# Hybrid decoder layer: product order in seven-product pairs, a smaller set of them, the store of h, and the spread of h's transposes

## The chip, the cores and the metric

The kernel runs on one core of a Trainium2 chip. The metric is the device time of one execution in microseconds (us), the median of several runs. Lower is better.

## The reference

The layer takes x of 256 rows by 2048 channels in float32 and computes

- `merged = sigmoid(g_A) * Up_A(FoX(xn)) + sigmoid(g_B) * Up_B(NSA(xn))`, with `xn = RMSNorm(x)` and two attention mixers FoX and NSA, all projected from xn by one matrix;
- `h = x + merged @ w_out` (w_out is 2048 x 2048);
- `y = h + (silu(hn @ w_gate) * (hn @ w_up)) @ w_down`, with `hn = RMSNorm(h)` and a hidden width of 5632.

The change lies in the second and third line. The first, which takes the first 640 us, it doesn't touch.

## The kernel before

**Precision.** Every matmul operand is split into hi (float32r, written by ScalarE with a copy) and lo (the remainder, written by VectorE with a subtraction). One product of a 128-wide block is then three matmuls of 128x512: hi by hi, hi by lo, lo by hi (lines 1066 to 1068, in `mac`).

**Pairs and units.** From the output projection on, the work is a list of units. A unit gives 256 rows by 1024 columns of output; it runs over `Pair`s, each with two 128-row blocks of the weight and the matching two blocks of the activation. That is a 2x2 by 2x2 block product. A plain pair (`mm_plain`) does it with eight block products into four sums (m2, m3, m4, c), so 24 matmuls; `mid` is called between its halves. A seven-product pair (`mm_seven`) uses the Winograd form: seven block products m1 to m7, so 21 matmuls, of which m1, m2 and m3 take plain blocks of the weight (part 0 of the split) and m5, m7, m6 and m4 take sums of blocks (part 1). The order of the seven is written out by hand: m1, m5, m7, m6, m2, m4, m3. m1, m5, m6 and m7 have four PSUM banks ("acc"), the others four more ("tp", printed as m in the profile). Transposes use acc banks too, when they are free.

**What the other engines do for a pair.** `Pair.load` issues two DMAs of 512 KB on SyncE's queue. `Pair.split` makes the parts: for a seven-product pair part 0 is three additions on VectorE (the sums, lines 1035 to 1038), then hi (line 1043, ScalarE) and lo (line 1044, VectorE) of three blocks; part 1 is hi and lo of the four sums. A plain pair has one part, hi and lo of four blocks. There are four part buffers, so the split of a part waits until TensorE has used the part four before it.

**After the last seven-product pair of a unit** `combine` reads m1 on ScalarE (line 1099) and m6, m7, m5 on VectorE (lines 1100 to 1103; m6 first) and so frees those banks. In the output units and the last down units `add_rows` then starts four DMAs on GpSimd's queue that add x (or h) to the four tiles in place (line 1135). After the unit's last pair `last` adds m2, m4, m3 and c to the tiles on VectorE (line 1112), and calls `done`.

**The two output units** (i = 0 and 1, 1024 columns of h each). Unit 0 takes the pairs in the order 1, 3, 0, 2, 5, 4, 6, 7, unit 1 from 0 to 7; pairs 0, 2 and 4 (`SW`) are seven-product ones. `done` is `h_evac`: the sum of squares of each tile, the store of h to `hacc` in DRAM (line 1162, on SyncE), and after unit 1 the second norm's scale `rh`, whose power runs on GpSimd (line 291).

**Transposes of h.** The gate/up units need h transposed, in eight pairs `hT[kp]`, made by `put_h`: four transposes of 128x128 on TensorE (line 996), then `put_seven` for kp 0, 2, 4 (lines 975 to 988) or `put_plain` for the others (hi on line 967, lo on line 968). Hooks say when: `(j, 0)` is before pair j of a unit and before the splits that are issued there, `(j, 1)` is between the halves of pair j. In unit 1 `(5, 0)` made kp 0 and 1 and `(5, 1)` kp 2 and 3; in the first gate/up unit `(3, 0)` made 4 and 5 and `(3, 1)` made 6 and 7. That first gate/up unit has pairs 0 and 2 as seven-product ones (`SH[:2]`), and pair 4 plain, on operands laid out for seven.

**The rest.** Eleven gate/up units in three groups (`GROUPS`), each group with two down units; down units of the first two groups accumulate into `hacc` by GpSimd's DMAs. The last group's first down unit takes its pairs in the order 0, 1, 2, 4, 3, 5, 6, 7, of which 0, 2 and 4 are seven-product ones.

**Order.** Nothing reorders the instructions: each engine runs its own in the order of the program. Before each pair the main loop calls the hook `pre`, then `run_ffn`, which issues loads and splits as far as buffers allow (three raw buffers, and parts of this and the next pairs up to `PARTS = 4`), then the products, then `combine` or `last`:

```python
if i >= ffn and ch.pre: ch.pre()
...
run_ffn(i)
...
ch.mm(ch)
...
if ch.done: ch.done()
```

Of the kernel before, what the change touches and what calls it, by code (L numbers as in the profile page):

```python
# [8 lines left out]
F32 = mybir.dt.float32  # L9
F32R = mybir.dt.float32r  # L10
AF = mybir.ActivationFunctionType
ALU = mybir.AluOpType
AX = mybir.AxisListType

P = 128
D = 2048
KB = D // P
T = 256
# [35 lines left out]
def hybrid_block(ctx: ExitStack, tc: tile.TileContext, x, norm_attn, w_in, fox_f_bias,  # L54
# [3 lines left out]
    nc = tc.nc  # L58
# [33 lines left out]
    def wk(shape, tag, bufs, dt=F32):  # L92
        pool = keep if tag in ("qs", "sm") else work
        return pool.tile(shape, dt, tag=tag, name=nm(tag), bufs=bufs)

    def bank(tag):
        tag = "acc" if tag == "acc" else "m"
        return psum.tile([P, 512], F32, tag=tag, name=nm(tag), bufs=4)
# [187 lines left out]
    def rstd_from(dst, ssq, n):  # L286

        w = ssq.shape[-1]
        v = wk([P, 16], "sm", 11)
        nc.vector.tensor_scalar(v[:, :w], ssq, 1.0 / n, EPS, op0=ALU.mult, op1=ALU.add)  # L290
        nc.gpsimd.tensor_tensor(dst, v[:, :w], nhalf[:, :w], op=ALU.pow)

    def row_ssq(dst, src):
        junk = wk([P, 512], "qs", 4)
        nc.scalar.activation(junk[:, :src.shape[-1]], src, AF.Square, accum_out=dst)
# [586 lines left out]
    mT = [None] * 8  # L882
    mtask, msrc = {}, {}
    SW = (0, 2, 4)
# [49 lines left out]
    def p3(shape, tag, bufs, dt=F32):  # L934
        return pools[3].tile(shape, dt, tag=tag, name=nm(tag), bufs=bufs)

    hacc = dram.tile([T, D], F32, name="hacc")
# [21 lines left out]
    def put_plain(dst, b, gains):  # L959
        if gains is None:  # L960
            d0, d1 = (dst[:, o].rearrange("p k t -> p (k t)") for o in range(2))
            nc.scalar.activation(d0, b, AF.Copy)
            nc.vector.tensor_tensor(d1, b, d0.bitcast(F32), op=ALU.subtract)
            return
        for k in range(2):
            hi, lo, src = dst[:, 0, k], dst[:, 1, k], b[:, k * T:(k + 1) * T]
            nc.scalar.activation(hi, src, AF.Copy, scale=gains[k])
            nc.vector.scalar_tensor_tensor(lo, src, gains[k], hi.bitcast(F32), op0=ALU.mult, op1=ALU.subtract)

    def put_seven(dst, b, gains):  # L970

# [79 lines left out]
    def unit(order, sevens, srcs, act, done, need, hooks=None, add=None):  # L1051


        hooks = hooks or {}
        plain = {(0, 0): "m2", (0, 1): "m3", (1, 0): "m4", (1, 1): "c"}
        total, seen, bk = {}, {}, {}
        for kp in order:
            for k in [f"m{j}" for j in range(1, 8)] if kp in sevens else list(plain.values()) * 2:
                total[k] = total.get(k, 0) + 1

        def mac(key, h, l, hi, lo):
            if key not in bk:
                bk[key] = bank("acc" if key in ("m1", "m5", "m6", "m7") else "tp")
            o, n = bk[key], seen.get(key, 0)
            seen[key] = n + 1
            nc.tensor.matmul(o, h, hi, start=n == 0, stop=False)  # L1066
            nc.tensor.matmul(o, h, lo, start=False, stop=False)  # L1067
            nc.tensor.matmul(o, l, hi, start=False, stop=n + 1 == total[key])  # L1068

        def mm_seven(ch):  # L1070
            a = act(ch.kp)
            o0 = a.shape[2] - 7
            for key, o, part, slot_ in (("m1", 0, 0, 0), ("m5", 3, 1, 0), ("m7", 4, 1, 1), ("m6", 5, 1, 2),
                                        ("m2", 1, 0, 1), ("m4", 2, 1, 3), ("m3", 6, 0, 2)):
                hi, lo = ch.op[part]
                mac(key, a[:, 0, o0 + o], a[:, 1, o0 + o], hi[:, slot_], lo[:, slot_])

        def mm_plain(ch):
            a = act(ch.kp)
            hi, lo = ch.op[0]  # L1080
            for c in range(2):
                if c and ch.mid:
                    ch.mid()
                for t in range(NT):
                    for k in range(2):
                        sl = ((1, 2), (0, 3))[c][k]
                        if a.shape[2] == 8:
                            ah, al = (a[:, o, ((1, 2), (0, 3))[t][k]] for o in range(2))
                        else:
                            ah, al = (a[:, o, k, t * P:(t + 1) * P] for o in range(2))  # L1090
                        mac(plain[t, c], ah, al, hi[:, sl], lo[:, sl])

        sb = {}

        def combine():

            (t1, t3), (u, w) = ([wk([P, 512], "qs", 4) for _ in range(2)], [p3([P, 512], "q2", 5) for _ in range(2)])
            tt, stt = nc.vector.tensor_tensor, nc.vector.scalar_tensor_tensor
            nc.scalar.activation(t1, bk["m1"], AF.Copy)
            tt(u, bk["m6"], t1, op=ALU.add)  # L1100
            tt(t3, bk["m7"], u, op=ALU.add)
            stt(w, bk["m5"], -1.0, t3, op0=ALU.mult, op1=ALU.subtract)
            stt(u, bk["m5"], -1.0, u, op0=ALU.mult, op1=ALU.subtract)
            for k in ("m1", "m5", "m6", "m7"):
                del bk[k]
            sb.update({(0, 0): t1, (0, 1): u, (1, 0): t3, (1, 1): w})
            if add:
                add(sb)

        def last():  # L1110
            for k in ((0, 0), (1, 0), (0, 1), (1, 1)):
                nc.vector.tensor_tensor(sb[k], bk[plain[k]], sb[k], op=ALU.add)
            done(sb)
            bk.clear()

        last7 = max(j for j, kp in enumerate(order) if kp in sevens)
        for j, kp in enumerate(order):
            def fin(j=j):
                if j == last7:
                    combine()  # L1120
                if j == len(order) - 1:
                    last()
            sv = kp in sevens
            pre, mid = hooks.get((j, 0)), hooks.get((j, 1))
            stream.append(Pair(unit, kp, sv, srcs(kp), mm_seven if sv else mm_plain, pre, mid, fin,
                               (lambda kp=kp: need(kp)) if need else None))

    def two(w, r0, c0):
        return lambda kp: [w[r0 + kp * 2 * P:r0 + (kp + 1) * 2 * P, c:c + 512] for c in (c0, c0 + 512)]
# [17 lines left out]
    def put_h(kp):  # L1147
        c = hs[kp // 4]
        k = kp // 2 % 2
        make = lambda kp: p3([P, 2, 8, P], "h7", len(SH), F32R) if kp in SH else p3([P, 2, 2, T], "hp", 8 - len(SH), F32R)  # L1150
        gains = [vecT[:, VF + 2 * kp + o:VF + 2 * kp + o + 1] for o in range(2)]
        hT[kp] = transpose_pair(make, [c[t, k] for t in range(NT)], kp % 2 * 256, kp, SH, gains, "acc")

    def put_hs(*kps):
        return lambda: [put_h(kp) for kp in kps]

    def h_evac(i):
        def done(c):
            hs[i] = dict(c)
            for t, h in ((0, 0), (1, 0), (0, 1), (1, 1)):  # L1160
                row_ssq(hss[:, t, 2 * i + h:2 * i + h + 1], c[t, h])
                nc.sync.dma_start(hacc[t * P:(t + 1) * P, (2 * i + h) * 512:(2 * i + h + 1) * 512], c[t, h])
            if i:
                s2 = wk([P, 16], "sm", 11)
                nc.vector.tensor_reduce(s2[:, :NT], hss, axis=AX.X, op=ALU.add)
                rstd_from(rh, s2[:, :NT], D)
        return done

    for i in range(2):
        unit((1, 3, 0, 2, 5, 4, 6, 7) if i == 0 else range(8), SW, two(w_out, 0, i * 1024), lambda kp: mT[kp], h_evac(i),  # L1170
             None if i else lambda kp: [mtask[j] for j in range(3)],
             {(5, 0): put_hs(0, 1), (5, 1): put_hs(2, 3)} if i else
             {(0, 1): put_m(5), (1, 0): put_m(6), (1, 1): put_m(7)}, add_rows(x, i * 1024))


# [49 lines left out]
    for g, (f0, f1) in enumerate(GROUPS):  # L1225
        n = 2 * (f1 - f0)
        order = list(range(n))
        more = g + 1 < len(GROUPS)

        for f in range(f0 + (1 if g else 0), f1 + (1 if more else 0)):  # L1230
            gate_up(f, transposes(f - 1, 5) if f > f0 + (1 if g else 0) else
                    {(3, 0): put_hs(4, 5), (3, 1): put_hs(6, 7)} if f == 0 else {})
        if more:
            down_unit(g, 0, order, {})
            down_unit(g, 1, order, transposes(f1, at[n]))
        else:
            down_unit(g, 0, [0, 1, 2, 4, 3, 5, 6, 7], transposes(f1 - 1, 4))
            down_unit(g, 1, order, {})
# [118 lines left out]
```

## Time and profile before

| | |
|---|---|
| runs, us | 1444.2, 1441.73, 1445.09 (median 1444.2) |
| profiled execution | 1444.2 us, span 1442.5 us, granted TensorE clock 0.997 |
| instructions | 18073, of them 6748 matmuls |
| moved by DMA | 287.06 MB, 199 GB/s in the mean |
| chain that ended last | TensorE 89%, VectorE 5%, ScalarE 2%, issue 2%, DMA 1% |

The span is from the first instruction to the last. The chain is followed back from the end: at each step to what released the waiting engine. In a row of a timeline the first number is the start in us from the span's start, the second the duration; where the engine stood idle before the instruction for longer, the idle time and what ended it stand in brackets at the end. Matmuls are pipelined, so the next starts before the row of the last ends. PE is TensorE, PEld its weight load, DVE VectorE, ACT ScalarE, POOL GpSimd, SP SyncE.

### The profile page before, as it was taken

The page shows a single profiled execution, that of the slowest core. Times are in us where ns is not written, and L with a number is a line of the kernel's source. Part 1 is how long each engine was busy: PE and PEld are TensorE (multiplying, and loading weights), DVE is VectorE, ACT ScalarE, POOL GpSimd, SP SyncE. Part 2 cuts the span into 40 slices and gives each one's busy share as a digit, 9 for nine tenths or more (in the row PEclk, how much of TensorE's full clock was granted, in tenths as well). Part 3 has the DMA queues.
Part 4 walks back from the last instruction along what each step waited for, and adds up shares of the span by engine and source line. Part 5 has one row for each costly group of instructions (what it writes and reads, how often), then busy time and mean ns, then how long its engine had stood idle before and what let it go on. Part 6 is the DMA issues. An engine that isn't in the chain of part 4 may idle for free.

```text
span 1442.5 us, 18073 instructions
## 1 busy us (share of the span) xinstructions
PE 1428.7 (99%) x6748; PEld 1199.5 (83%) x6748; DVE 1137.3 (79%) x1458; ACT 762.2 (53%) x949; POOL 62.4 (4%) x75
## 2 busy tenths in 40 slices
PE   9999999999999999999999999999999999999998
PEld 7888888999888888888778888888888888888787
DVE  7766766776776646669888999888899988889975
ACT  6466554455667444454655555455555555555542
POOL 2001010000000000000000000010000000000000
PEclk9999999999999999999999999999999999999999
DMA  7576876456443666566865666679565577856585
GB/s 279 175 233 198 268 237 184 129 173 208 148 125 117 195 198 187 180 210 194 257 214 175 205 204 207 201 210 257 175 205 187 197 218 216 257 179 199 179 245 136
DMA packets 156419, 287.06 MB, mean 199 GB/s; under 512 B 9598, under 2 KB 32220, under 8 KB 156204
## 3 DMA queue, kind: packets, MB, share of 16 engines
q1 hardware_dynamic: 151260, 275.87, 60.1%
q0 software_dynamic: 4896, 9.78, 4.0%
q8 instruction: 53, 0.87, 0.2%
q10 hardware_dynamic: 176, 0.27, 0.1%
q14 instruction: 34, 0.28, 0.1%
HBM read 277.48 MB, written 8.40 MB: 198 GB/s over the span
## 4 chain that ended last, share of the span: by engine, by line
PE 89%; DVE 5%; ACT 2%; issue 2%; DMA 1%; POOL 0%; SPq 0%; ACTq 0%; DVEq 0%; POOLq 0%
PE acc L193 12%; PE acc L194 12%; PE acc L195 12%; PE m L1068 12%; PE m L1067 12%; PE m L1066 12%; PE acc L1067 3%; PE acc L1068 3%; PE acc L1066 3%; DVE lo L1044 2%; ACT hi L1043 2%; DMA q<-in_x_dram 1%; DVE sums L1035 1%; PE acc L996 1%; PE m L536 1%
## 5 line engine op out<-in xcount | busy, mean ns | idle before, releaser
L171 DVE TENSOR_TENSOR lo<-raw,hi 128x1024 fp32r<-128x1024 f32 (+5 forms) x229 | 267.5, 1172 | 138.7 <-ACT hi L170 138.5
L1044 DVE TENSOR_TENSOR lo<-raw,hi 128x2048 fp32r<-128x2048 f32 (+1 forms) x148 | 309.1, 2092 | 42.9 <-ACT hi L1043 42.7
L193 PE MATMUL acc<-hi,u 128*128 128x512 f32 (+4 forms) x832 | 322.7, 388 | 0.0
L194 PE MATMUL acc<-lo,u 128*128 128x512 f32 (+4 forms) x832 | 316.9, 381 | 0.4 <-DVE lo L171 0.4
L195 PE MATMUL acc<-hi,u 128*128 128x512 f32 (+4 forms) x832 | 317.0, 381 | 0.0
L170 ACT ACTIVATE hi<-raw 128x1024 fp32r<-128x1024 f32 (+5 forms) x229 | 229.3, 1018 | 151.5 <-PE acc L195 138.9
L1043 ACT ACTIVATE hi<-raw 128x2048 fp32r<-128x2048 f32 (+1 forms) x148 | 257.1, 1752 | 93.0 <-PE m L1068 68.0
L1043 ACT ACTIVATE hi<-sums 128x2048 fp32r<-128x2048 f32 x54 | 103.7, 1920 | 170.1 <-DVE sums L1038 134.2
L195 PEld LDWEIGHTS acc<-hi,u 128*128 128x128 f32 x832 | 156.4, 188 | 27.2
L194 PEld LDWEIGHTS acc<-lo,u 128*128 128x128 f32 x832 | 156.7, 188 | 25.3 <-DVE lo L171 0.9
L193 PEld LDWEIGHTS acc<-hi,u 128*128 128x128 f32 x832 | 156.6, 188 | 24.6 <-ACT hi L170 0.2
L1066 PE MATMUL m<-hi,hp 128*128 128x512 f32 x440 | 172.9, 393 | 0.0
L1068 PE MATMUL m<-hi,hp 128*128 128x512 f32 x440 | 171.5, 390 | 0.0
L1067 PE MATMUL m<-lo,hp 128*128 128x512 f32 x440 | 171.3, 389 | 0.0
L1044 DVE TENSOR_TENSOR lo<-sums,hi 128x2048 fp32r<-128x2048 f32 x54 | 123.7, 2291 | 25.7 <-ACT hi L1043 25.7
L1068 PEld LDWEIGHTS m<-hi,hp 128*128 128x128 f32 x440 | 82.6, 188 | 17.3
L1067 PEld LDWEIGHTS m<-lo,hp 128*128 128x128 f32 x440 | 82.7, 188 | 16.8
L1066 PEld LDWEIGHTS m<-hi,hp 128*128 128x128 f32 x440 | 82.6, 188 | 16.6
L1066 PE MATMUL m<-hi,u 128*128 128x512 f32 x210 | 82.8, 394 | 0.0
L1068 PE MATMUL m<-hi,u 128*128 128x512 f32 x210 | 82.1, 391 | 0.0
L1067 PE MATMUL m<-lo,u 128*128 128x512 f32 x210 | 82.0, 390 | 0.0
L1035 DVE TENSOR_TENSOR sums<-raw 128x1024 f32<-128x1024 f32 x54 | 65.8, 1218 | 0.0
(305 smaller groups left out, 1974.8 us busy)
## 6 DMA issues: line engine op xcount, KB each, us to landing
raw<-in_w_in_dram SPq DMA_DIRECT2D x127, 512.0 KB
raw<-in_w_ffn_gate_dram SPq DMA_DIRECT2D x88, 512.0 KB
raw<-in_w_ffn_up_dram SPq DMA_DIRECT2D x88, 512.0 KB
raw<-in_w_ffn_down_dram SPq DMA_DIRECT2D x88, 512.0 KB
raw<-in_w_out_dram SPq DMA_DIRECT2D x32, 512.0 KB
raw<-in_w_in_dram SPq DMA_DIRECT2D x24, 384.0 KB
raw<-in_w_up_fox_dram SPq DMA_DIRECT2D x16, 512.0 KB
raw<-in_w_up_nsa_dram SPq DMA_DIRECT2D x16, 512.0 KB
```

Source lines behind the costliest of these rows:

```text
L170: nc.scalar.activation(hi[:, :m], ch.raw[:, :m], AF.Copy)
L171: nc.vector.tensor_tensor(lo[:, :m], ch.raw[:, :m], hi[:, :m].bitcast(F32), op=ALU.subtract)
L193: nc.tensor.matmul(o, h, ch.hi[:, j], start=first and j == 0, stop=False)
L194: nc.tensor.matmul(o, h, ch.lo[:, j], start=False, stop=False)
L195: nc.tensor.matmul(o, l, ch.hi[:, j], start=False, stop=last and j == w - 1)
L536: nc.tensor.matmul(o, s, ch.hi[:, j], start=j == 0, stop=False)
L1035: nc.vector.tensor_tensor(s[:, 0:2], w[:, 0].unsqueeze(1).to_broadcast([P, 2, 512]), w[:, 1:4:2], op=ALU.add)
L1043: nc.scalar.activation(h, src, AF.Copy)
L1044: nc.vector.tensor_tensor(l, src, h.bitcast(F32), op=ALU.subtract)
L1066: nc.tensor.matmul(o, h, hi, start=n == 0, stop=False)
L1067: nc.tensor.matmul(o, h, lo, start=False, stop=False)
L1068: nc.tensor.matmul(o, l, hi, start=False, stop=n + 1 == total[key])
```

## The change

Five edits, all behind the attention part:

- `put_plain`, where gains are given (h's transposes): both hi are issued, then both lo.
- `mm_seven`: where the unit already has products, the order is m1, m2, m3, m5, m7, m6, m4; for a unit's first pair it stays.
- Output unit 0: pairs 0 and 2 are seven-product ones, pair 4 is plain. Its operand keeps the layout for seven, which `mm_plain` can read.
- `put_hs(kp, j)` gives four hooks: kp before pair j, kp+1 in its middle, kp+2 before pair j+1, kp+3 in its middle. Unit 1 has kp 0 to 3 at pairs 5 and 6; the first gate/up unit kp 4 to 7 at pairs 3 and 4.
- `h_evac`: the eight stores of h go on GpSimd's queue.

```diff
@@ put_plain
+        src = [b[:, k * T:(k + 1) * T] for k in range(2)]
         for k in range(2):
-            hi, lo, src = dst[:, 0, k], dst[:, 1, k], b[:, k * T:(k + 1) * T]
-            nc.scalar.activation(hi, src, AF.Copy, scale=gains[k])
-            nc.vector.scalar_tensor_tensor(lo, src, gains[k], hi.bitcast(F32), op0=ALU.mult, op1=ALU.subtract)
+            nc.scalar.activation(dst[:, 0, k], src[k], AF.Copy, scale=gains[k])
+        for k in range(2):
+            nc.vector.scalar_tensor_tensor(dst[:, 1, k], src[k], gains[k], dst[:, 0, k].bitcast(F32),
+                                           op0=ALU.mult, op1=ALU.subtract)
@@ mm_seven
-            for key, o, part, slot_ in (("m1", 0, 0, 0), ("m5", 3, 1, 0), ("m7", 4, 1, 1), ("m6", 5, 1, 2),
-                                        ("m2", 1, 0, 1), ("m4", 2, 1, 3), ("m3", 6, 0, 2)):
+
+            for key in ("m1 m2 m3 m5 m7 m6 m4" if seen else "m1 m5 m7 m6 m2 m4 m3").split():
+                o, part, slot_ = {"m1": (0, 0, 0), "m2": (1, 0, 1), "m3": (6, 0, 2), "m4": (2, 1, 3),
+                                  "m5": (3, 1, 0), "m6": (5, 1, 2), "m7": (4, 1, 1)}[key]
                 hi, lo = ch.op[part]
                 mac(key, a[:, 0, o0 + o], a[:, 1, o0 + o], hi[:, slot_], lo[:, slot_])
@@ put_hs
-    def put_hs(*kps):
-        return lambda: [put_h(kp) for kp in kps]
+    def put_hs(kp, j):
+
+        return {(j + o // 2, o % 2): lambda o=o: put_h(kp + o) for o in range(4)}
@@ h_evac
-                nc.sync.dma_start(hacc[t * P:(t + 1) * P, (2 * i + h) * 512:(2 * i + h + 1) * 512], c[t, h])
+                nc.gpsimd.dma_start(hacc[t * P:(t + 1) * P, (2 * i + h) * 512:(2 * i + h + 1) * 512], c[t, h])
@@ the output units
-        unit((1, 3, 0, 2, 5, 4, 6, 7) if i == 0 else range(8), SW, two(w_out, 0, i * 1024), lambda kp: mT[kp], h_evac(i),
+        unit(range(8) if i else (1, 3, 0, 2, 5, 4, 6, 7), SW if i else SW[:2], two(w_out, 0, i * 1024), lambda kp: mT[kp], h_evac(i),
              None if i else lambda kp: [mtask[j] for j in range(3)],
-             {(5, 0): put_hs(0, 1), (5, 1): put_hs(2, 3)} if i else
+             put_hs(0, 5) if i else
@@ the gate/up units
-                    {(3, 0): put_hs(4, 5), (3, 1): put_hs(6, 7)} if f == 0 else {})
+                    {} if f else put_hs(4, 3))
```

## Rows read from the trace of the kernel before

**Rows 1.** The page's first part: busy us (share of the span), instructions

```profile
PE 1428.7 (99%) x6748; PEld 1199.5 (83%) x6748; DVE 1137.3 (79%) x1458; ACT 762.2 (53%) x949; POOL 62.4 (4%) x75
```

**Rows 2.** Timeline, TensorE, first and second output unit: start, us, engine, line, op, count, [idle]

```profile
655.46 0.39 PE L1068 MATMUL acc<-hi,u 128*128 128x512 f32 x1
655.96 0.50 PE L1066 MATMUL acc<-hi,u 128*128 128x512 f32 x1
...
697.92 0.50 PE L1067 MATMUL acc<-lo,u 128*128 128x512 f32 x1 [1.62 <-DVE lo L1044]
```

**Rows 3.** Timeline, TensorE, second output unit to first gate/up unit

```profile
707.34 0.39 PE L1066 MATMUL acc<-hi,u 128*128 128x512 f32 x1
...
709.84 0.39 PE L1068 MATMUL acc<-hi,u 128*128 128x512 f32 x1
...
730.22 0.39 PE L1066 MATMUL acc<-hi,h 128*128 128x512 f32 x1
...
731.44 0.49 PE L1066 MATMUL acc<-hi,h 128*128 128x512 f32 x1 [0.38 <-ACT hi L1043]
733.76 0.50 PE L1067 MATMUL acc<-lo,h 128*128 128x512 f32 x1 [1.83 <-DVE lo L1044]
...
746.52 0.50 PE L1067 MATMUL acc<-lo,h 128*128 128x512 f32 x1 [0.67 <-DVE lo L1044]
...
751.53 0.66 PE L996 MATMUL acc<-ident,qs 128*128 128x128 f32 x4 [0.38 <-DVE q L1100]
```

**Rows 4.** Timeline, TensorE, last group's first down unit

```profile
1368.53 0.50 PE L1067 MATMUL acc<-lo,u 128*128 128x512 f32 x1 [1.73 <-DVE lo L1044]
...
1369.35 0.63 PE L1067 MATMUL acc<-lo,u 128*128 128x512 f32 x1
...
1372.75 0.40 PE L1066 MATMUL m<-hi,u 128*128 128x512 f32 x1
```

**Rows 5.** Windows: stretch, length, busy (x) of PE, PEld, DVE, ACT, POOL, PEclk, DMA, GB/s

```profile
684.60:730.20 45.60, 43.93 (x200) 35.85 (x200) 38.78 (x43) 24.96 (x31) 3.43 (x4) 1.00 0.85 257
734.00:738.50 4.50, 4.50 (x14) 3.43 (x14) 4.30 (x5) 1.96 (x7) 0.00 (x0) 0.62 0.30 60
738.50:751.00 12.50, 11.83 (x54) 9.37 (x52) 11.34 (x10) 8.03 (x8) 1.63 (x1) 1.00 0.79 247
1369.00:1373.00 4.00, 4.00 (x13) 3.10 (x12) 4.00 (x3) 1.24 (x2) 0.00 (x0) 0.57 0.60 199
```

**Rows 6.** Timeline, VectorE, first output unit to first gate/up unit

```profile
690.25 0.69 DVE L1112 TENSOR_TENSOR q<-m,q 128x512 f32<-128x512 f32 x1 [1.36 <-DMA q<-in_x_dram]
...
695.57 2.29 DVE L1044 TENSOR_TENSOR lo<-sums,hi 128x2048 fp32r<-128x2048 f32 x1 [0.38 <-ACT hi L1043]
...
711.75 0.68 DVE L1100 TENSOR_TENSOR q<-acc,qs 128x512 f32<-128x512 f32 x1
...
717.87 0.48 DVE L968 SCALAR_TENSOR_TENSOR hp<-acc,vecT,hp 128x256 fp32r<-128x256 f32 x1 [0.55 <-ACT hp L967]
...
719.67 2.29 DVE L1044 TENSOR_TENSOR lo<-raw,hi 128x2048 fp32r<-128x2048 f32 x1 [1.32 <-ACT hi L1043]
...
731.41 2.29 DVE L1044 TENSOR_TENSOR lo<-sums,hi 128x2048 fp32r<-128x2048 f32 x1 [1.32 <-ACT hi L1043]
...
735.83 0.68 DVE L1112 TENSOR_TENSOR qs<-m,qs 128x512 f32<-128x512 f32 x1
```

**Rows 7.** Timeline, VectorE, last group's first down unit

```profile
1366.18 2.29 DVE L1044 TENSOR_TENSOR lo<-sums,hi 128x2048 fp32r<-128x2048 f32 x1 [0.40 <-ACT hi L1043]
```

**Rows 8.** The page's fifth part, VectorE's sums: count, busy, mean ns, idle

```profile
L1044 DVE TENSOR_TENSOR lo<-sums,hi 128x2048 fp32r<-128x2048 f32 x54 | 123.7, 2291 | 25.7 <-ACT hi L1043 25.7
L1035 DVE TENSOR_TENSOR sums<-raw 128x1024 f32<-128x1024 f32 x54 | 65.8, 1218 | 0.0
```

**Rows 9.** Timeline, GpSimd's DMA issues and VectorE beside them

```profile
676.54 1.22 DVE L1035 TENSOR_TENSOR sums<-raw 128x1024 f32<-128x1024 f32 x1
...
677.13 2.03 POOL L1135 DMA_DIRECT2D q<-in_x_dram  x2
```

## The prediction

> **What bounds the kernel now.** Start with the page's busy times: TensorE works through 99% of the span and VectorE is second [rows 1]. So a change can win in two ways only: fewer products, or fewer microseconds in which TensorE stands still. I then went through the timeline of TensorE from the first output-projection unit to the end, looking at the starts. Undisturbed 128x512 matmuls start 0.227 us apart (eleven steps from 707.34 to 709.84 [rows 3]), and the row of one is 0.39 us long, so a wait costs its printed idle time plus 0.16 us. Wherever starts are further apart, time is lost. There are few such places, and nearly all stand in a burst of 100 us around the two output-projection units and the first gate/up unit [rows 2, 3], with one more in the last group's first down unit [rows 4]. Third, the granted clock by stretch: after the two largest of these losses TensorE ran with 0.62 of its full clock for a few microseconds, and it did not after the loss at 697.92 [rows 5]. Fourth, the timeline of VectorE through the same 100 us, to see what was late [rows 6].
>
> The losses, each from its rows: 655.46 to 655.96 is 0.50 where 0.23 is due, 0.27 lost; at 697.92, 1.62 + 0.16 = 1.78 [rows 2]. At the first pair of the first gate/up unit 0.38 + 0.16 = 0.54 for hi and then 1.83 + (0.49 - 0.23) = 2.09 for lo, together 2.63; at that unit's third pair 0.67 + 0.16 = 0.83; at its transposes 0.38 [rows 3]. In the last group 1.73 + 0.16 = 1.89, and then eight starts at half clock, 1369.35 to 1372.75, take 3.40 where 8 x 0.227 = 1.81 do, 1.59 lost [rows 4]. The gate/up unit has the same slow stretch behind its 2.63 [rows 5]; I price it at 1.59 too. Sum: 0.27 + 1.78 + 2.63 + 1.59 + 0.83 + 0.38 + 1.89 + 1.59 = 10.96 us. That is all the change can reach, and all of it hangs on VectorE or on buffers that VectorE frees late.
>
> **The change, part by part.** All is summed against the profiled execution, 1444.2 us with a span of 1442.5; it is also the median of the three runs.
>
> *Two seven-product pairs in the first output-projection unit.* Row pair 4 becomes plain: eight block products in place of seven, three matmuls more, 3 x 0.227 = **0.68 us added** to TensorE. VectorE loses the sums' three additions (the first alone 1.22 us) and a lo pass: two passes, the sums' of 2.29 among them, become one of that size [rows 8]. The larger effect is on combine. It now comes after the fourth pair, not the sixth, so x's accumulating DMAs start two plain pairs (10.9 us) sooner. Before, VectorE stood before the unit's last additions for x to land, 1.36 us at 690.25; the sums behind them were late, then the lo at 695.57, then TensorE at 697.92 [rows 2, 6]. Now x lands at about 690.25 - 10.9 = 679.3, ahead of the unit's end near 685 (45 matmuls before the pair that waited), and the last of four additions starts near 687. From its start to the end of that lo were 697.86 - 690.25 = 7.6 us, so the lo ends at 694.6. TensorE asks for it at 697.92 - 1.78 + 0.68 - 0.27 and, by the next edit, 1.36 later, 697.9: **1.78 goes**.
>
> *Plain-block products first.* In every pair with products before it in its unit, m1, m2, m3 go first and the products of the sums follow. The sums' lo is wanted six matmuls later, 6 x 0.227 = 1.36 us. At 655.96 it was m6 that waited, for a bank that a transpose held; it moves behind m2 and m3, and **0.27 goes**. In the last group the lo of the sums ended where the wait did [rows 4, 7]; nothing before it on VectorE changes, so **1.36 of 1.89 goes, 0.53 stays**. A remainder so short I take to leave the clock alone, for behind the 0.83 at 746.52 the stretch has 1.00 [rows 5]: **1.59 goes**. What it may cost: m6, which combine needs first, ends 1.36 us later. Its last matmul started at 709.84, ran 0.39, and VectorE took it up at 711.75 [rows 3, 6], so it lay finished for 1.52 and still does for 0.16. I take nothing; the upper end is 1.36 in each of the two chains where VectorE is late, 2.7 together. Below nothing it could help only by freeing the plain parts' buffers 2.7 us sooner, which the same waits already count.
>
> *Transposes spread, and both hi before both lo.* In the second output unit the four transposed pairs of h went into one plain pair; now each half of two pairs has one. I follow VectorE in the changed unit. All of it is earlier by what was won so far, 0.27 + 1.78 - 0.68 = 1.37, since its work there is paced by buffers that TensorE frees: the last plain lo before combine waits for the fourth pair. So combine starts at 711.75 - 1.37 = 710.38. From there to the first addition at 735.83 VectorE took 24.08 us [rows 6]. In a plain put each lo waited for its hi and the second hi for the first lo, an inner pause of 0.55 [rows 6], twice; with both hi first these go, and the two pauses of 1.32 before a split shrink to about 1.2 by the rows' ends. That is 1.4 saved: additions from 735.83 - 1.37 - 1.4 = 733.06. The lo of the sums of the first gate/up pair gains more, because the fourth put now stands behind it: 1.5 for that put (two lo of 0.48 and the pause), 0.55 and 2 x 0.12 for the other pauses, 2.3. It ends at 733.7 - 1.37 - 2.3 = 730.0. TensorE reaches that unit at 730.22 - 1.37 = 728.85 and wants the lo four matmuls later at 729.76: **0.3 is left of 2.63**. But then TensorE gets to m2 at 728.85 + 0.3 + 12 x 0.227 = 731.87, and m2's bank is freed by the first addition, at 733.06 + 0.68 = 733.7. **A new wait of 1.85** takes the place; in the trace of before the long stop hid it. Ends: 0 if VectorE is 1.9 us quicker than I have it, 2.63 + 1.59 if the puts save nothing. The third pair's lo ends at 746.52 - 1.37 - 1.4 = 743.75; TensorE, at 728.85 + 0.3 + 1.85 + 45 x 0.227 + 10 x 0.227 = 743.5, waits **0.3 in place of 0.83**. The second transpose of that unit moves from the pair's start to its middle, 12 matmuls later: **0.38 goes**.
>
> The clock is the open point of this part. After 1.78 lost in one piece it stayed at 1.00, after 2.63 with one matmul between it fell, after 1.89 it fell [rows 2 to 5]. What I forecast is 0.3, nine matmuls, then 1.85. By size it lies between; the nearest single stop is the 1.78. I take no slow stretch; with it the unit loses 1.59 and the 0.3 behind it vanishes, 1.3 net.
>
> *h stored by GpSimd's queue.* SyncE loses eight store issues that stood among weight loads until the additions were done; no wait in the trace names a late weight load, so nothing is gained. On GpSimd's queue they stand before the power that gives the second norm's scale, which is first wanted at the end of the gate/up unit, eight pairs later, and before accumulations far behind. They are covered; uncovered, four issues cost 4 us. Two of its DMA issues took 2.03 us while VectorE ran a sums addition in 1.22 us, its mean over all 54 [rows 8, 9]: no sign that one held the other.
>
> The Trainium skill, SBUF — State Buffer, "Summary: rules for kernel authors", says to keep a DMA that is to hide under VectorE off GpSimd's queue, because the two share an SBUF port pair and one blocks the other. [...]
>
> **Sum.** Left or added: 0.68 + 0.53 + 0.3 + 1.85 + 0.3 = 3.66. Gain 10.96 - 3.66 = 7.3; 1444.2 - 7.3 = **1436.9 us**.
>
> **Rivals.** *Slower: the stores hold VectorE.* Eight issues at about 1.0 us each [rows 9] fall at the ends of the two output units, just where VectorE is last. If each stops VectorE for its length, it is 4 us late twice; TensorE waits each time, and the clock falls each time: 8 + 2 x 1.59 = 11.2 against 7.3 won, 1444.2 + 3.9 = **1448.1**. It decides from 10.2 us of loss on. Against it: the undisturbed addition of rows 9. Chance 0.04.
>
> The Trainium skill's page SBUF — State Buffer, "Who interferes with whom", states the port lock behind this rival for VectorE instructions with two SBUF inputs against GpSimd's reads; rows 9 do not show it.
>
> *No change: the waits come back.* VectorE remains late in the first gate/up unit and in the last group: the full 2.15 with a slow stretch (3.74), and in the last group m6's lateness pushes the lo by 1.36, so 1.89 and 1.59 stay. Gain: 1.37 + (4.22 - 3.74) + 0.83 + 0.38 = 3.1, and if the third pair still waits 0.83, 2.2: **1442.0**. For it: VectorE is second only to TensorE and has no idle time in these chains. Against: m6 has 0.16 in hand, and the last group's chain begins before any moved instruction. Chance 0.10.
>
> *All waits go.* VectorE catches up by 2 us: 10.96 - 0.68 = 10.3, **1433.9**. Chance 0.16. That the edits do nothing to the program is excluded, for each changes an order or a queue.
>
> **How the numbers follow.** My forecast, with or without the slow stretch (1436.9 or 1438.2), 0.70. The range goes from the best case, 1433.9, to the third, and 1.4 lower, since the runs of before lie 3.4 us apart: 1432.5 to 1441.6. Faster by over 0.2% (2.9 us, about what a measurement can tell) is the forecast and the best case, 0.86; within it the no-change case, 0.10; slower 0.04.
>
> **What would show it.** No wait near 655, 697 and 751; at the first gate/up unit a wait of about 0.3 for lo and one near 1.9 before m2, released by the additions; half a microsecond in the last group with the clock at 1.00; combine still without idle time before it; weight loads and VectorE's durations unchanged. I would be wrong if combine waited for m6, if a sums addition grew under GpSimd's issues, or if waits appeared in units that had none.

## The result, and the profile after

The changed kernel takes 1435.84 us in the median of five runs (1435.7 to 1436.6) where the kernel before took 1443.87 (1441.73 to 1445.09). The two medians are 8.0 us apart. The ratio of the runs is 0.9949, with a 95% interval of 0.9935 to 0.9964: by it the changed kernel is 7.4 us faster, 5.2 to 9.4. The forecast was 1436.9, and all five runs lie in its range. The profiled execution took 1435.8 us, with a span of 1434.1.

The page of the changed kernel, its first part and the chain that ended last:

```profile
PE 1424.9 (99%) x6751; PEld 1197.7 (84%) x6751; DVE 1132.0 (79%) x1454; ACT 760.4 (53%) x948; POOL 66.8 (5%) x83
...
PE 94%; DVE 3%; ACT 1%; issue 1%; DMA 0%; POOL 0%; SPq 0%; ACTq 0%; DVEq 0%; POOLq 0%
```

There are three matmuls more than before, VectorE is 5 us less busy [rows 1], and TensorE's share of the chain is up from 89% to 94%: less of the path now runs through VectorE.

Next the changed kernel's timeline of TensorE: the first matmul of the first output unit, and then every place behind it where it stood for 0.2 us or more. The same statements stand two to five lines further down in this kernel than in the one before.

```profile
641.19 0.39 PE L1068 MATMUL m<-hi,u 128*128 128x512 f32 x1
...
730.92 0.40 PE L1070 MATMUL acc<-hi,h 128*128 128x512 f32 x1
...
732.76 0.50 PE L1068 MATMUL m<-hi,h 128*128 128x512 f32 x1 [1.45 <-DVE qs L1116]
...
742.98 0.50 PE L1069 MATMUL acc<-lo,h 128*128 128x512 f32 x1
...
1360.39 0.50 PE L1069 MATMUL acc<-lo,u 128*128 128x512 f32 x1 [0.23 <-DVE lo L1046]
...
1363.08 0.50 PE L1069 MATMUL acc<-lo,u 128*128 128x512 f32 x1 [0.36 <-DVE lo L1046]
```

Of the waits of before [rows 2 to 4] those near 656, 698 and 751 are gone. The first gate/up unit has one long wait, before m2, for the first of the unit's additions (line 1116 here): 732.76 - 730.92 - 0.23 = 1.61 us. Its third pair waits 0.30 (742.98, the wait so short that the row has no bracket; the matmul before started at 742.45). The last group has two short waits, 0.39 and 0.52.

From the first output unit's first matmul to the end are 1434.1 - 641.19 = 792.9 us; before it was 1442.5 - 641.30 = 801.2. I use that stretch below to compare traces, since the attention part's length differs by up to 1.6 us from trace to trace, in code that no edit touches.

The granted clock (the column after POOL's count) behind the longest wait, by windows of the changed kernel:

```profile
728.60:732.80 4.20, 2.75 (x13) 1.73 (x11) 4.20 (x6) 0.78 (x2) 0.00 (x0) 1.00 0.00 0
732.80:737.00 4.20, 4.20 (x18) 3.45 (x19) 3.04 (x6) 4.03 (x9) 3.15 (x5) 1.00 0.87 247
```

It stays at 1.00 (2.4 GHz); before it fell to 0.62 in this place [rows 5].

VectorE through the same stretch, and one of the new store issues on GpSimd's queue:

```profile
671.68 1.23 DVE L1037 TENSOR_TENSOR sums<-raw 128x1024 f32<-128x1024 f32 x1 [0.98 <-DMA raw<-in_w_out_dram]
...
684.36 0.68 DVE L1116 TENSOR_TENSOR qs<-m,qs 128x512 f32<-128x512 f32 x1
...
686.53 0.54 POOL L1167 DMA_DIRECT2D hacc<-q  x1
686.75 1.21 DVE L1037 TENSOR_TENSOR sums<-raw 128x1024 f32<-128x1024 f32 x1
...
691.47 2.29 DVE L1046 TENSOR_TENSOR lo<-sums,hi 128x2048 fp32r<-128x2048 f32 x1 [0.38 <-ACT hi L1045]
...
709.63 0.68 DVE L1104 TENSOR_TENSOR q<-acc,qs 128x512 f32<-128x512 f32 x1
...
726.83 2.29 DVE L1046 TENSOR_TENSOR lo<-sums,hi 128x2048 fp32r<-128x2048 f32 x1 [1.12 <-ACT hi L1045]
...
732.02 0.68 DVE L1116 TENSOR_TENSOR qs<-m,qs 128x512 f32<-128x512 f32 x1
```

The additions at 684.36 no longer stand before a DMA; the sums behind them start at 686.75 where they started right after the addition of 690.25 [rows 6], and their lo ends at 693.76, not 697.86. From combine (709.63) to the next unit's first addition (732.02) are 22.4 us where there were 24.1. The sums' addition beside the store issue takes 1.21 us, as ever. One thing is new: at 671.68 VectorE waited 0.98 us for a weight load. x's accumulating transfers now lie in that stretch. TensorE did not stand still there.

### The profile page after: what moved, and what is told of

It reads as the page before. It is cut to its first block, busy times and chain, and to the rows that moved or that the text cites. A ratio compares the mean times of both kernels' runs of the same rounds, so it can differ in the third digit from the quotient of the medians.

```text
span 1434.1 us, 18111 instructions
## 1 busy us (share of the span) xinstructions
PE 1424.9 (99%) x6751; PEld 1197.7 (84%) x6751; DVE 1132.0 (79%) x1454; ACT 760.4 (53%) x948; POOL 66.8 (5%) x83
## 4 chain that ended last, share of the span: by engine, by line
PE 94%; DVE 3%; ACT 1%; issue 1%; DMA 0%; POOL 0%; SPq 0%; ACTq 0%; DVEq 0%; POOLq 0%
PE m L1070 13%; PE m L1068 13%; PE m L1069 13%; PE acc L193 13%; PE acc L195 13%; PE acc L194 13%; PE acc L1069 3%; PE acc L1070 3%; PE acc L1068 3%; DVE lo L1046 1%; PE acc L998 1%; ACT hi L1045 1%; PE m L536 1%; PE m L537 1%; PE m L372 0%
## 5 line engine op out<-in xcount | busy, mean ns | idle before, releaser
L1068 PE MATMUL m<-hi,u 128*128 128x512 f32 x215 | 84.3, 392 | 0.0
L1070 PE MATMUL m<-hi,u 128*128 128x512 f32 x215 | 83.8, 390 | 0.0
```

## The experiments

The theory on trial: TensorE's time is lost where it waits for VectorE, each edit takes away the waits that the prediction named for it, and the store matters to nobody. Rivals: the smaller set of seven-product pairs frees VectorE and is the real source, the order only shifting waits; or the store's move is (by freeing SyncE, or on the other side by holding VectorE). First each edit alone on the kernel before, then each taken back from the changed kernel, then three steps further. A difference under some 2 us between two medians can't be trusted alone, because the kernel before itself had medians of 1440.9 to 1443.9 in different sets of runs; so small ones are read from the waits in the traces, and times are given as ratios to the kernel before on the same chip. The changed kernel was timed in the set of the result alone, so a difference between its ratio, 0.9949, and one from another set carries that scatter too.

### The order alone

```diff
-            for key, o, part, slot_ in (("m1", 0, 0, 0), ("m5", 3, 1, 0), ("m7", 4, 1, 1), ("m6", 5, 1, 2),
-                                        ("m2", 1, 0, 1), ("m4", 2, 1, 3), ("m3", 6, 0, 2)):
+            for key in ("m1 m2 m3 m5 m7 m6 m4" if seen else "m1 m5 m7 m6 m2 m4 m3").split():
```

> The kernel before with the product order alone. Theory (TensorE waits for VectorE's lo of the sums, and a product asked for 6 matmuls later waits 1.36 us less): gone are 0.27 at 655.96, 1.36 of the 1.78 at 697.92, the 0.83 at 746.52, 1.36 of 1.89 in the last group and its slow stretch of 1.59; the waits of 0.54 and 2.09 at the first gate/up unit and the slow stretch behind them stay. Gain 5.4 us against the kernel before. Rival (the smaller set of seven-product pairs is what freed VectorE, and the order only shifts waits about): gain under 1.5 us.

Ratio 0.9965 (0.9952 to 0.9979), 5.0 us faster. The timeline of TensorE in this run has these waits left, besides 0.45 for a hi just before the first; then the clock behind that first one:

```profile
731.75 0.50 PE L1067 MATMUL acc<-lo,h 128*128 128x512 f32 x1 [1.82 <-DVE lo L1044]
...
749.08 0.66 PE L996 MATMUL acc<-ident,qs 128*128 128x128 f32 x4 [0.93 <-ACT F L978]
...
1365.73 0.50 PE L1067 MATMUL acc<-lo,u 128*128 128x512 f32 x1 [0.35 <-DVE lo L1044]
```

```profile
731.50:736.00 4.50, 4.25 (x12) 3.30 (x13) 4.50 (x6) 1.47 (x5) 0.00 (x0) 0.62 0.20 30
```

The waits near 656, 697 and 746 are gone and the last group's is 0.51. The first gate/up unit keeps its wait of 2.1, with half-clock starts behind it, and the idle time before its transposes is 0.93 where it was 0.38. So the theory holds, and more went than was due: at 697 not 1.36 but all of 1.78. Here the last of x's transfers had landed 11.0 us after GpSimd began to issue the last two, in the profile of before after 13.1; that differs from run to run (10.7 to 13.8 in five traces).

### Two seven-product pairs in the first output unit alone

```diff
-        unit((1, 3, 0, 2, 5, 4, 6, 7) if i == 0 else range(8), SW, two(w_out, 0, i * 1024), lambda kp: mT[kp], h_evac(i),
+        unit((1, 3, 0, 2, 5, 4, 6, 7) if i == 0 else range(8), SW if i else SW[:2], two(w_out, 0, i * 1024), lambda kp: mT[kp], h_evac(i),
```

> The kernel before with two seven-product pairs in the first output unit alone. Theory: three matmuls add 0.68, the 1.78 at 697.92 goes because x lands in time, 0.3 at 688.95 goes; the waits at the first gate/up unit and in the last group stay as they were. Gain 1.4 us. Rival (less work for VectorE pulls the whole chain ahead): the waits at the first gate/up unit shrink too, gain 4 us or more.

Ratio 0.9990 (0.9981 to 0.9999), 1.4 us faster, as the theory said. The longest waits of TensorE that it leaves, and the clock by windows:

```profile
732.59 0.50 PE L1067 MATMUL acc<-lo,h 128*128 128x512 f32 x1 [1.83 <-DVE lo L1044]
...
735.39 0.50 PE L1066 MATMUL m<-hi,h 128*128 128x512 f32 x1 [0.67 <-DVE qs L1112]
...
745.62 0.50 PE L1067 MATMUL acc<-lo,h 128*128 128x512 f32 x1 [1.55 <-DVE lo L1044]
...
1367.39 0.50 PE L1067 MATMUL acc<-lo,u 128*128 128x512 f32 x1 [1.73 <-DVE lo L1044]
```

```profile
730.20:735.00 4.80, 2.64 (x9) 1.61 (x9) 4.76 (x3) 1.80 (x2) 0.00 (x0) 1.00 0.00 0
735.00:740.00 5.00, 4.61 (x20) 3.85 (x21) 4.06 (x8) 3.97 (x9) 1.55 (x1) 1.00 0.82 211
1369.00:1373.00 4.00, 4.00 (x22) 3.28 (x20) 3.96 (x4) 1.05 (x3) 0.36 (x1) 1.00 0.56 179
```

The 1.78 is gone, and the first gate/up unit is no better off: the rival falls. Two things are to be seen here. In this execution the clock stayed at 1.00 behind the same two waits that were followed by half clock in the profile of before. And with the clock up, TensorE reached m2 before the addition had freed its bank and waited 0.83 there (735.39), and at the third pair 1.71 instead of 0.83. What the clock had cost, the buffers cost instead: VectorE sets the pace in this unit.

### The puts alone (spread, and both hi before both lo)

```diff
-             {(5, 0): put_hs(0, 1), (5, 1): put_hs(2, 3)} if i else
+             put_hs(0, 5) if i else
...
-                    {(3, 0): put_hs(4, 5), (3, 1): put_hs(6, 7)} if f == 0 else {})
+                    {} if f else put_hs(4, 3))
```

(with `put_hs` and `put_plain` as in the changed kernel)

> The kernel before with the transposes spread and both hi before both lo, nothing else. Theory: at the first gate/up unit 2.63 of waiting and the slow stretch become one wait of about 1.9 before m2 at full clock, the bank wait of 0.38 goes, the third pair's wait grows from 0.83 to about 1.5 because TensorE is there sooner. Gain 1.8 us. Rival (the spread is worth nothing by itself since VectorE's work is the same): gain under 0.5 us.

Ratio 0.9987 (0.9978 to 0.9996), 1.9 us faster. TensorE's waits in the first gate/up unit:

```profile
735.89 0.50 PE L1068 MATMUL m<-hi,h 128*128 128x512 f32 x1 [1.49 <-DVE qs L1114]
...
745.85 0.50 PE L1069 MATMUL acc<-lo,h 128*128 128x512 f32 x1 [1.27 <-DVE lo L1046]
```

1.65 before m2 (1.9 expected) and 1.44 at the third pair (1.5), none before the transposes. The wait before m2 thus comes without the other three edits. It is not made by the puts alone, for with the smaller set alone TensorE stood 0.83 for the same bank, behind the longer stop for lo.

### The store alone

```diff
-                nc.sync.dma_start(hacc[t * P:(t + 1) * P, (2 * i + h) * 512:(2 * i + h + 1) * 512], c[t, h])
+                nc.gpsimd.dma_start(hacc[t * P:(t + 1) * P, (2 * i + h) * 512:(2 * i + h + 1) * 512], c[t, h])
```

> The kernel before with h stored by GpSimd's queue alone. Theory: no weight load was late behind the stores, and GpSimd's issues hold nobody: within 0.3 us of the kernel before, VectorE's operations beside the issues as long as before. Rival one (SyncE's loads were held): faster by 1 us or more. Rival two (the issues hold VectorE): slower by several us, additions and lo passes longer beside them.

Ratio 0.9997 (0.9987 to 1.0006): nothing that can be measured, and a gain over 1.9 us or a loss over 0.9 is outside the interval. Timeline of VectorE and GpSimd at the end of the first output unit:

```profile
687.09 0.54 POOL L1162 DMA_DIRECT2D hacc<-q  x1
...
688.09 0.69 DVE L1112 TENSOR_TENSOR q<-m,q 128x512 f32<-128x512 f32 x1 [1.30 <-DMA q<-in_x_dram]
688.70 1.22 DVE L1035 TENSOR_TENSOR sums<-raw 128x1024 f32<-128x1024 f32 x1
```

The addition before and the sums behind the issues have their usual lengths. The wait near 697 is 0.75 in this trace, not 1.78, because x landed sooner. The store need not be the reason: x's transfers are issued before the first store, and with the store on SyncE the last one landed 11.0 to 13.8 us after the issue in three traces, here after 11.7.

### The order taken back from the changed kernel

```diff
-            for key in ("m1 m2 m3 m5 m7 m6 m4" if seen else "m1 m5 m7 m6 m2 m4 m3").split():
+            for key, o, part, slot_ in (("m1", 0, 0, 0), ("m5", 3, 1, 0), ("m7", 4, 1, 1), ("m6", 5, 1, 2),
+                                        ("m2", 1, 0, 1), ("m4", 2, 1, 3), ("m3", 6, 0, 2)):
```

> The changed kernel with the old order of the seven products. Theory: waits asked for 1.36 us earlier come back: 0.37 near 655, the third pair of the first gate/up unit 0.3 to about 1.7, the last group 0.85 to 1.9 with a slow stretch of 1.6; the wait before m2 stays at 1.6. Slower than the changed kernel by 4.3 us. Rival (the order only shifts waits): under 1 us.

Ratio 0.9985 (0.9976 to 0.9994) where the changed kernel has 0.9949: 5.2 us are lost by the ratios, 2.6 in the two traces' stretch from the first output unit on (795.5 against 792.9). TensorE's waits and the clock behind the second:

```profile
743.70 0.50 PE L1069 MATMUL acc<-lo,h 128*128 128x512 f32 x1 [1.24 <-DVE lo L1046]
...
1365.01 0.50 PE L1069 MATMUL acc<-lo,u 128*128 128x512 f32 x1 [1.72 <-DVE lo L1046]
```

```profile
1366.00:1370.00 4.00, 4.00 (x21) 3.31 (x20) 3.96 (x4) 1.08 (x3) 0.00 (x0) 1.00 0.58 183
```

0.26 near 656, 1.39 at the third pair and 1.89 in the last group are back, as expected but for the slow stretch. That the ratios say twice what the traces say is not explained; the two ratios are from different sets. Each edit alone on the kernel before, the order is the largest part of the gain: 5.0 us, against 1.9 for the puts, 1.4 for the smaller set and nothing for the store.

### Three seven-product pairs in the first output unit again

```diff
-        unit(range(8) if i else (1, 3, 0, 2, 5, 4, 6, 7), SW if i else SW[:2], two(w_out, 0, i * 1024), lambda kp: mT[kp], h_evac(i),
+        unit(range(8) if i else (1, 3, 0, 2, 5, 4, 6, 7), SW, two(w_out, 0, i * 1024), lambda kp: mT[kp], h_evac(i),
```

> The changed kernel with three seven-product pairs in the first output unit again. Theory: three matmuls fewer, so 0.68 less; x lands late again, which costs 0.3 near 688 and 1.78 less 1.36 near 697, together about 0.8 with what follows each wait: within 0.4 us of the changed kernel. Rival (the smaller set is a main part of the gain): slower by 1.8 us or more.

Ratio 0.9954 (0.9937 to 0.9971), not to be told from the changed kernel's; by the traces it is 1.3 us shorter (791.7 against 792.9), of which 0.68 are the three matmuls; the short waits of the changed kernel, 0.30 at the third pair and 0.39 in the last group, are not there. Its rows of VectorE and TensorE:

```profile
687.08 0.69 DVE L1116 TENSOR_TENSOR q<-m,q 128x512 f32<-128x512 f32 x1 [0.23 <-DMA q<-in_x_dram]
```

```profile
732.33 0.50 PE L1068 MATMUL m<-hi,h 128*128 128x512 f32 x1 [1.50 <-DVE qs L1116]
...
1362.15 0.50 PE L1069 MATMUL acc<-lo,u 128*128 128x512 f32 x1 [0.36 <-DVE lo L1046]
```

No wait near 688 or 697: with the new order the lo is asked for 1.36 later, and x came soon enough in this run. So beside the new order this edit only guards against a late x, at the price of three matmuls.

### Two puts at a hook again, hi still first

```diff
-             put_hs(0, 5) if i else
+             {(5, 0): put_hs(0, 1), (5, 1): put_hs(2, 3)} if i else
```

(and the same in the first gate/up unit)

> The changed kernel with two puts at each hook again, both hi still before both lo. Theory: the lo of the sums of the first gate/up pair stands behind the fourth put again and ends 0.9 us later, a wait of about 0.7; the wait before m2 shrinks by as much, since the additions come at the same time; the bank wait of 0.4 comes back. Slower by 0.4 us. Rival (the spread carries the gain in that unit): slower by 2 us or more.

Ratio 0.9966 (0.9953 to 0.9979), an interval that overlaps the changed kernel's; 793.4 against 792.9 us by the traces. TensorE:

```profile
729.32 0.50 PE L1069 MATMUL acc<-lo,h 128*128 128x512 f32 x1 [0.65 <-DVE lo L1046]
...
732.13 0.50 PE L1068 MATMUL m<-hi,h 128*128 128x512 f32 x1 [0.69 <-DVE qs L1116]
...
746.50 0.66 PE L998 MATMUL acc<-ident,qs 128*128 128x128 f32 x4 [0.93 <-ACT F L980]
```

A wait of 0.80 for lo, then 0.85 before m2, in sum what the one wait of 1.61 was: the additions come when they come, and for these two waits the spread only chooses where TensorE stands. The bank wait before the transposes is back too, with 0.93 of idle time and not the 0.4 that I expected.

### The plain puts as hi, lo, hi, lo

```diff
...
-        for k in range(2):
-            nc.scalar.activation(dst[:, 0, k], src[k], AF.Copy, scale=gains[k])
         for k in range(2):
+            hi, lo, src = dst[:, 0, k], dst[:, 1, k], b[:, k * T:(k + 1) * T]
+            nc.scalar.activation(hi, src, AF.Copy, scale=gains[k])
...
```

> The changed kernel with hi, lo, hi, lo in the plain puts again. Theory: each of the two puts before the additions holds VectorE for a pause of 0.55 more, so the wait before m2 grows from 1.6 to about 2.7; slower by 1.1 us, and by 2.7 if the clock falls behind it. Rival (the puts are covered): no difference.

Ratio 0.9991 (0.9982 to 1.0000) against 0.9949: 6 us lost, 3.6 by the traces (796.5 against 792.9). More than expected. The timelines of ScalarE, TensorE and VectorE, and the clock:

```profile
722.67 0.47 ACT L967 ACTIVATE hp<-acc,vecT 128x256 fp32r<-128x256 f32 x1 [5.28 <-DVE hp L968]
...
730.08 0.47 ACT L967 ACTIVATE hp<-acc,vecT 128x256 fp32r<-128x256 f32 x1 [2.40 <-DVE hp L968]
```

```profile
729.70 0.50 PE L1067 MATMUL acc<-lo,h 128*128 128x512 f32 x1 [0.60 <-DVE lo L1044]
...
735.33 0.50 PE L1066 MATMUL m<-hi,h 128*128 128x512 f32 x1 [3.18 <-DVE qs L1114]
```

```profile
709.40 0.68 DVE L1102 TENSOR_TENSOR q<-acc,qs 128x512 f32<-128x512 f32 x1
...
732.38 2.29 DVE L1044 TENSOR_TENSOR lo<-raw,hi 128x2048 fp32r<-128x2048 f32 x1 [1.32 <-ACT hi L1043]
...
734.59 0.68 DVE L1114 TENSOR_TENSOR qs<-m,qs 128x512 f32<-128x512 f32 x1
```

```profile
735.40:740.50 5.10, 5.10 (x16) 4.06 (x17) 3.87 (x8) 3.99 (x9) 3.85 (x5) 0.67 0.92 276
```

From combine to the first addition VectorE needs 25.2 us, not 22.4. Spread, a put stands in the middle of VectorE's splits, so its first lo is reached late; the second hi waits for that lo, 5.28 us, and all of ScalarE's queue stands behind it. Most of VectorE's loss, 2.0 of the 2.8, falls at the second of these puts: there the hi of the next split stands behind the put's second hi on ScalarE, and VectorE waits 1.32 for it (732.38), a wait that the changed kernel does not have and I did not expect. Spread without hi first is a loss, for the order alone, without any edit to the puts, has 0.9965 (0.9952 to 0.9979) and 794.7 us by its trace; hi first without the spread, in the run before this one, does nearly as well as both.

### The store on SyncE again

```diff
-                nc.gpsimd.dma_start(hacc[t * P:(t + 1) * P, (2 * i + h) * 512:(2 * i + h + 1) * 512], c[t, h])
+                nc.sync.dma_start(hacc[t * P:(t + 1) * P, (2 * i + h) * 512:(2 * i + h + 1) * 512], c[t, h])
```

> The changed kernel with h stored by SyncE again. Theory: within 0.3 us of the changed kernel. Rival one (the stores on SyncE hold the weight loads): slower by 1 us or more. Rival two (GpSimd's issues hold VectorE): faster.

Ratio 0.9948 (0.9933 to 0.9963), the changed kernel's. TensorE:

```profile
733.11 0.50 PE L1068 MATMUL m<-hi,h 128*128 128x512 f32 x1 [1.47 <-DVE qs L1116]
...
1362.89 0.50 PE L1069 MATMUL acc<-lo,u 128*128 128x512 f32 x1 [0.35 <-DVE lo L1046]
```

The wait before m2 is 1.63 and the last group's second one 0.51, as in the changed kernel; its two short ones, 0.30 at the third pair and 0.39 in the last group, are under 0.2 here. By the traces the run is 0.6 us shorter (792.35 against 792.91). So the store's queue makes no difference that can be told, from either side.

### m6 straight behind m3

```diff
-            for key in ("m1 m2 m3 m5 m7 m6 m4" if seen else "m1 m5 m7 m6 m2 m4 m3").split():
+            for key in ("m1 m2 m3 m6 m7 m5 m4" if seen else "m1 m5 m7 m6 m2 m4 m3").split():
```

> The changed kernel with m6 before m7 and m5 behind m3 (m1, m2, m3, m6, m7, m5, m4). Theory: combine's first addition waited 0.2 us for m6 in the changed kernel and no longer does, so VectorE is some 0.3 earlier in every unit; the waits in the last group shrink by that, from 0.4 and 0.5 to about 0.1 and 0.2, the rest stays: faster by 0.5 us. Rival (that wait is hidden): no difference.

Ratio 0.9955 (0.9941 to 0.9968): no difference. In the changed kernel combine of the unit before the last group's down units started 0.20 late, which I took for a wait for m6:

```profile
1327.44 0.69 DVE L1104 TENSOR_TENSOR q<-acc,qs 128x512 f32<-128x512 f32 x1 [0.20 <-issue]
```

The same row in the run before this one, the store on SyncE, which has the changed kernel's order; then this run, VectorE and TensorE:

```profile
1327.25 0.68 DVE L1104 TENSOR_TENSOR q<-acc,qs 128x512 f32<-128x512 f32 x1
```

```profile
1327.05 0.68 DVE L1104 TENSOR_TENSOR q<-acc,qs 128x512 f32<-128x512 f32 x1
```

```profile
1360.14 0.50 PE L1069 MATMUL acc<-lo,u 128*128 128x512 f32 x1
...
1362.84 0.50 PE L1069 MATMUL acc<-lo,u 128*128 128x512 f32 x1 [0.36 <-DVE lo L1046]
```

The 0.20 is gone, and the first of the two waits is 0.25 in place of 0.39; the second is 0.52 as before. But the 0.20 is gone as well with the store on SyncE, where m6 stands where it did, and the 0.39 is under 0.2 in all six other traces with the changed kernel's order. The row of the changed kernel names no engine as the releaser, and by its own row m6's last matmul had ended 0.4 us earlier. So no run shows that m6 comes late for combine. My expectation of 0.5 was a miss.

### Two seven-product pairs in the second output unit too

```diff
-        unit(range(8) if i else (1, 3, 0, 2, 5, 4, 6, 7), SW if i else SW[:2], two(w_out, 0, i * 1024), lambda kp: mT[kp], h_evac(i),
+        unit(range(8) if i else (1, 3, 0, 2, 5, 4, 6, 7), SW[:2], two(w_out, 0, i * 1024), lambda kp: mT[kp], h_evac(i),
```

> The changed kernel with two seven-product pairs in the second output unit as well. Theory: three matmuls add 0.68; VectorE loses 4.3 us of work ahead of the first gate/up unit, so the wait of 1.6 before m2 and the 0.3 behind it go, with 0.1 after each: faster by 1.4 us. Rival (the wait is set by the puts and the additions, not by the amount of work): slower by 0.7 us.

1434.11 us (1433.31 to 1434.37), ratio 0.9939 (0.9927 to 0.9952): 1.4 us under the changed kernel's ratio, with intervals that overlap, and 2.0 shorter by the traces (790.9). The store on SyncE, which was timed in the same set, took 1434.91 to 1435.59, more than any of these five runs. Only one wait of TensorE over 0.2 us is left behind the attention part:

```profile
1361.51 0.50 PE L1069 MATMUL acc<-lo,u 128*128 128x512 f32 x1 [0.36 <-DVE lo L1046]
```

The wait before m2 was a matter of the amount of VectorE's work ahead of it. Three matmuls, 0.68 us, buy off 1.61 and 0.30; the 0.39 in the last group is not there either.

### All three further steps

The edits of the last two, and two seven-product pairs in the last group's first down unit:

```diff
-        unit(order, SD[2 * (f1 - f0)], two(w_ffn_down, f0 * 512, i * 1024),
+        unit(order, SD[2 * (f1 - f0)][:2 if final and not i else 3], two(w_ffn_down, f0 * 512, i * 1024),
```

> The changed kernel with two seven-product pairs in the second output unit, the order of o_m6, and two seven-product pairs in the last group's first down unit. Theory: the 1.4 of b_unit1; in the last group 0.68 added and the waits of 0.4 and 0.5 with what follows them gone, 0.4 won; faster by 1.8 us in all, and no wait over 0.2 us left from the first output unit on. Rival (further cuts of VectorE's work buy nothing and the added matmuls stay): slower by 1.4 us.

1433.6 us (1433.47 to 1434.67), ratio 0.9939 (0.9926 to 0.9951), 790.7 by the trace. No wait over 0.2 us is left from the first output unit on. It is faster than the kernel before. Its interval overlaps the changed kernel's, than which it is 2.2 shorter by the traces; against the run before it the difference (0.2 in the traces) is too small to call.

## Why the prediction was right

**The result.** 7.3 us were forecast and 7.4 measured, by the mechanism named. Every wait that was to go is gone, and the one that was to come came where it was placed. That the two numbers lie so close is partly luck: 3.18 of the 7.3 were two slow stretches that the kernel before need not have in every run, and what the sum left out went the other way.

**The losses of before.** The list of waits held. The 1.59 for each slow stretch did not, as a property of the kernel. The last group's wait of 1.89 appears in full in four experiments (the smaller set alone, the puts alone, the store alone, the order taken back), and in none of these did the clock fall behind it; behind the 2.1 of the first gate/up unit it fell in two of the three experiments that keep it. The profiled execution had caught both, which may be one reason why it lies 1.3 us above the 1442.88 that the kernel before had in 26 runs. In the profiles the gain is 8.4, by the ratio of the runs 7.4.

**Two seven-product pairs.** The price of 0.68 and the mechanism (x lands in time; lo's end forecast at 694.6, measured 693.76) were right. The credit was not: I gave this edit the whole 1.78 near 697. By the order alone it goes too, and with the order in place taking this edit back costs nothing. In both of those traces, though, x landed 11.0 and 10.7 us after its issue, not 13.1 as in the trace of before; what the edit is worth beside the order when x is that late, no run shows. Alone it is worth 1.4.

**Plain-block products first.** 0.27, the third pair's share and 1.36 of the last group's 1.89 were to go; 0.53 was to stay, and 0.52 did. I took m6's lateness at nothing, and no run shows that it costs anything. A wait of 0.39 appeared in the last group that the sum did not have; the six other traces with the same order do not have it, and its cause stays open.

**The puts.** The additions were forecast at 733.06 and came at 732.02, the combine at 710.38 and came at 709.63: the chain between was forecast as 22.7 us and took 22.4. The wait before m2 was to be 1.85 and is 1.61; the lo before it, to be waited for by 0.3, was in time; the third pair's wait of 0.3 is 0.30. The clock stayed up behind the 1.61 in all six traces that have it (the changed kernel, the puts alone, and four others), as I had read from the 1.78. The credit between the two edits to the puts was mis-sized: the sum gave hi first two inner pauses of 0.55, but with the puts spread it saves 2.8 us of VectorE's chain, 25.2 against 22.4. In the sum both edits were taken together, so that this cancelled.

**The store.** Nothing forecast, nothing measured, alone and taken back. The rival that the issues hold VectorE would have shown as longer or later additions: they took 1.21 and 1.22 us beside the issues, against a mean of 1.22 [rows 8], and started with no idle time before them. The Trainium skill (SBUF — State Buffer, "Who interferes with whom") has a VectorE instruction with two SBUF inputs contend with a GpSimd instruction that reads SBUF; no run here shows such a block.

**What the sum left out.** Each wait is followed by a matmul that starts 0.1 us late, and x's lateness cost 0.3 near 689. By my estimate from the rows that is about 1.1 us in the trace of before and 0.5 in the changed kernel's, one part of what the profiles' 8.4 has over the forecast's 7.3; the 0.39 lies against it. Two smaller slips stand in the prediction: the bank wait was taken at its printed 0.38, without the 0.16 that its own rule adds, and the range's upper end, 1441.6, is not the 1442.0 of the case that it is said to come from. Neither changes the result.

## What to carry to other kernels

Where two engines are nearly level, list each place where the faster one stands and ask what it was asked for, and when: here six matmuls of work that needs less, put ahead of work that needs more, were worth more (5.0 us alone) than taking work away (1.4 alone, and 2.0 by the traces in the second output unit). Follow the helper's queue past the wait that you remove, up to the next buffer that it frees; the new wait of 1.6 us could be worked out beforehand from the old trace, as 1.85, and its cure from the new one. Spreading a step over a queue changes what its inner waits hold up, so look again at the order inside the step.

## What the runs showed that was not expected

TensorE's half-clock stretches (0.57 to 0.67 by the windows, eight or so starts of 0.43 us) do not follow from the length of a wait alone. A wait of 1.9 us was followed by one in the profile of before and by none in four other traces; waits of 2.6 us in all by one in three traces of four; a wait of 3.35 by one in the only trace that has it; waits of 1.6 in none of six. Nor do such stretches stand behind these waits alone: in six of the fourteen traces the clock also fell in the first 20 us of the span, to 0.91 over that stretch, in code that no edit touches. The runs of the kernel before are spread over 3.4 us, those of the changed one over 0.9. It is tempting to put this down to the stretches, of some 1.5 us each, but it is not shown: two runs of the puts alone with the same granted clock, 1.0, took 1438.36 and 1441.62 us.

The other is the time from the issue of x's last two accumulating transfers to the landing of the last one, 10.7 to 13.8 us for the same 256 KB each. On it hung a wait that was 1.8 in two traces and 0.75 in another, in code that is the same up to there.
